# One level of Strassen's algorithm for gate and up of a SwiGLU in 17 of 22 blocks, with down blocks between a group's runs

## The chip, the cores and the metric

The kernel runs on one core of a Trainium2 chip. The metric is the device time of one execution in microseconds (us). Short names: PE is TensorE (matmuls), PEld its weight loads, DVE is VectorE, ACT is ScalarE, POOL is GpSimd, SP is the engine that issues the DMAs. PSUM is the memory that matmuls write to; one bank holds 128 x 512 float32.

## The reference, cut to what matters

One residual block over 512 tokens of width 1024 in float32. The change concerns the last two lines, the SwiGLU with its hidden width of 2816 and the final norm:

```python
def _rms(t, w):
    y = t * lax.rsqrt(jnp.mean(t * t, axis=-1, keepdims=True) + EPS)
    return y * w

def _swiglu(h, w_gate, w_up, w_down):
    return (jax.nn.silu(h @ w_gate) * (h @ w_up)) @ w_down

x = x + _mixer_block(_rms(x, norm_mix_w), ...)          # attention, gated linear attention
x = x + _memory_xattn(_rms(x, norm_mem_q_w), _rms(mem, norm_mem_kv_w), ...)
x = x + _swiglu(_rms(x, norm_ffn_w), w_ffn_gate, w_ffn_up, w_ffn_down)
return _rms(x, norm_final_w)
```

## The kernel before

**Layout.** All activations are transposed: features on the 128 partitions, the 512 tokens along the free axis. The residual stream is eight tiles `res[0]` to `res[7]` of 128 x 512 (named `x` in the profile). The hidden width is 22 blocks of 128 features.

**Two parts for each number.** Every float32 operand is split (`split`, lines 93 to 104) into a high part, a cast on ACT to the format that matmuls read, and a low part, the rest, a subtraction on DVE. `prod3` makes three matmuls of a product: high by high, high by low, low by high. A unit (`unit`) is a weight tile of 128 x 1024: a DMA brings it into `R`, ACT casts it to `H`, DVE leaves the rest in `L`. There are three buffers for each of the three, so the cast of a unit waits for the run that last read its buffer, and the DMA of a unit for the low part of the one three before.

**The FFN, lines 1008 to 1060.** For each hidden block j, `block` makes a run of 24 matmuls of 512 columns (8 blocks of the width by 3) for gate into the bank `pg`, and another run for up into `pu`. `ps_mm` has four banks, so a run can start when the bank of four runs ago has been read. The 1/rms of each token isn't in the operands `zh`, `zl`; it is multiplied in behind the matmuls by `n2.b`, a 128 x 512 tile with the same row in each partition (`rb` in the profile). So each block has on DVE L1022 (gate by 1/rms, out of PSUM), on ACT the Silu, on DVE L1024 (by up, out of PSUM) and L1025 (by 1/rms), and a split. The norm `n2` runs beside the first blocks: squares on ACT, their sums on DVE (L205), a matmul with ones (`t`), a chain of small operations on DVE for the inverse root (L216, L166 to L178; its end is `rt`), a matmul that spreads it over the partitions, and a copy on ACT into `rb`.

Behind the 22 blocks come the eight blocks of the down product, one for each `res[j]`: 66 matmuls of 512 columns each (22 by 3), an addition to `res[j]` (L1040), the squares for the final norm `n3`, and a product with the final gain. The last one is made in two halves of 256 tokens, each with its own `n3.finish` and its eight products into `fin` (L1052 to L1058; six on DVE, two on POOL), which go out by DMA. `finish` and its spread share a single PSUM bank (`ps_t`), and L1052 and L1058 read the spread from it.

**Order.** Each engine executes its own instructions in the order in which the program issues them; across engines they wait for each other through semaphores. The compiler's scheduler chose the order on each engine here.

Of the kernel before, what the change touches and what calls it, by code (L numbers as in the profile page):

```python
# [11 lines left out]
F32 = mybir.dt.float32  # L12
# [17 lines left out]
NEG = -1.0e30  # L30
TGW = 328
DENSE = (10, 5, 11, 3, 1)


def build(tc, a, out):
# [11 lines left out]
    cp = ctx.enter_context(pool("cp"))  # L47


    edge = ctx.enter_context(pool("ep", side="right")).tile([P, 24], F32, name="edge")  # L50
# [30 lines left out]
    def f(ap):  # L81
        return ap.bitcast(F32)
# [97 lines left out]
    class Norm:  # L180
# [23 lines left out]
            else:  # L204
                nc.vector.tensor_tensor(out=acc, in0=acc, in1=sq, op=ALU.add)  # L205

        def finish(self, spread=True, cols=None):
# [7 lines left out]
            v = cp.tile([P, nt], F32, name=uniq(f"v_{self.name}"))  # L215
            nc.vector.tensor_scalar(  # L216
                out=v, in0=ps[:, 0 : 2 * nt].rearrange("p (t c) -> p t c", c=2)[:, :, 0],
                scalar1=1.0 / D, scalar2=EPS, op0=ALU.mult, op1=ALU.add,
            )
# [785 lines left out]
    mep_ctx.__exit__(None, None, None)  # L1005


    fp_ctx = pool("fp")
    fp = fp_ctx.__enter__()
    ah = [fp.tile([P, S], F32R, name=f"ah{j}") for j in range(NF)]  # L1010
    al_ = [fp.tile([P, S], F32R, name=f"al{j}") for j in range(NF)]
    for j in range(NF):
        pg = ps_mm()
        block(pg, [(unit(a["w_fg"][j]), KC)], zh, zl)
        pu = ps_mm()
        block(pu, [(unit(a["w_fu"][j]), KC)], zh, zl)
        if j == 0:
            for i in range(KC):
                n2.add(res[i])
            n2.finish()  # L1020
# [5 lines left out]
        split(ah[j], al_[j], t)  # L1026

    n3 = Norm("n3", S)
    for j in range(KC):
        units = []  # L1030
        for k0 in range(0, NF, KC):
            nk_ = min(KC, NF - k0)
            units.append((unit(a["w_fd"][j][:, k0 * P : (k0 + nk_) * P]), nk_))
# [100 lines left out]
```

## Time and profile before

| | |
|---|---|
| time, median of 3 runs | 918.81 us (918.31 to 920.23) |
| the profiled execution's own time | 919.91 us |
| its span, first to last instruction | 918.1 us |
| mean granted TensorE clock | 0.995 |
| PE busy | 901.2 us, 98% of the span |
| DVE busy | 557.4 us, 61% |
| ACT busy | 426.5 us, 46% |
| first FFN matmul, end of the last gate or up run, start of the second half of the last block | 541.7, 783.2, 896.4 us |

The profile is of one execution; its times below are on its own clock, which starts with the first instruction. Busy times overlap between engines. A row of a timeline gives the start, the duration, the line, the operation and, in brackets, the idle time before it on its engine with what ended it. A duration of one instruction is longer than the distance to the next where instructions overlap; the distance between starts is called the pace here.

### The profile page before, as it was taken

The numbers are of one execution on the slowest core, as the hardware profiler recorded it, in microseconds if no ns is written. First come the engines' busy times: TensorE is split into PE (matmuls) and PEld (weight loads), VectorE is DVE, ScalarE is ACT, GpSimd is POOL, SyncE is SP. The second block draws the span as 40 slices with busy tenths as digits, with TensorE's granted clock in tenths as the row PEclk, the third lists the DMA queues.
The fourth block names the chain that finished last, engine by engine and source line by source line (L and its number), as shares of the span: only waits on it lengthen the run. The fifth ranks groups of instructions, "written<-read, shape, count | busy, mean of one in ns | idle before, by whom it ended". The sixth has DMA issues, their size and how long they took to land.

```text
span 918.1 us, 11424 instructions
## 1 busy us (share of the span) xinstructions
PE 901.2 (98%) x4318; PEld 746.7 (81%) x4318; DVE 557.4 (61%) x1104; ACT 426.5 (46%) x760; POOL 7.0 (1%) x30
## 2 busy tenths in 40 slices
PE   8999999999999999999999999999999999999995
PEld 6898888887888787778888778888888888888885
DVE  6777888777343959966766996444444444323323
ACT  7576574556333838463445864223332233222220
POOL 1000000000000000000000000000000000000001
PEclk9999999999999999999999999999999999999998
DMA  7232221222232031425432222232222322323212
GB/s 249 92 115 70 69 70 69 70 69 69 92 96 89 23 115 48 143 86 161 114 115 92 70 89 95 94 107 99 92 92 92 106 100 86 104 86 103 87 41 92
DMA packets 29415, 86.11 MB, mean 94 GB/s; under 512 B 4048, under 2 KB 7760, under 8 KB 29360
## 3 DMA queue, kind: packets, MB, share of 16 engines
q1 hardware_dynamic: 29216, 85.37, 28.9%
q8 instruction: 34, 0.56, 0.2%
q14 instruction: 21, 0.17, 0.1%
q10 hardware_dynamic: 144, 0.00, 0.0%
HBM read 83.27 MB, written 2.10 MB: 93 GB/s over the span
## 4 chain that ended last, share of the span: by engine, by line
PE 89%; DVE 6%; ACT 3%; DMA 1%; issue 1%; SPq 0%; DVEq 0%; ACTq 0%
PE mm L79 80%; PE s L79 3%; PE o L79 3%; PE t L79 1%; DVE L L98 1%; PE t L545 1%; ACT pm L93 1%; DMA R<-in_w_tg 1%; PE mm L545 1%; ACT H L97 1%; DVE sl L98 1%; DVE on L747 1%; DMA x<-in_xT 0%; PE t L758 0%; DVE st L706 0%
## 5 line engine op out<-in xcount | busy, mean ns | idle before, releaser
L97 ACT CAST H<-R 128x1024 fp32r<-128x1024 f32 (+2 forms) x155 | 156.8, 1013 | 326.1 <-PE mm L79 247.0
L98 DVE TENSOR_TENSOR L<-R,H 128x1024 fp32r<-128x1024 f32 (+2 forms) x155 | 181.8, 1174 | 93.9 <-ACT H L97 93.5
L79 PE MATMUL mm<-xl,H 128*128 128x512 f32 x592 | 232.3, 392 | 0.0
L79 PE MATMUL mm<-xh,L 128*128 128x512 f32 x592 | 232.1, 392 | 0.0
L79 PE MATMUL mm<-xh,H 128*128 128x512 f32 x592 | 230.6, 390 | 0.0
L79 PEld LDWEIGHTS mm<-xh,H 128*128 128x128 f32 x592 | 111.2, 188 | 22.5
L79 PEld LDWEIGHTS mm<-xl,H 128*128 128x128 f32 x592 | 111.2, 188 | 22.1
L79 PEld LDWEIGHTS mm<-xh,L 128*128 128x128 f32 x592 | 111.3, 188 | 21.7
L79 PE MATMUL mm<-ah,H 128*128 128x512 f32 (+1 forms) x198 | 72.5, 366 | 0.0
L79 PE MATMUL mm<-ah,L 128*128 128x512 f32 (+1 forms) x198 | 72.4, 366 | 0.0
L79 PE MATMUL mm<-al,H 128*128 128x512 f32 (+1 forms) x198 | 72.4, 365 | 0.0
L79 PE MATMUL mm<-H,xh 128*128 128x512 f32 (+1 forms) x192 | 70.3, 367 | 0.0
L79 PE MATMUL mm<-L,xh 128*128 128x512 f32 (+1 forms) x192 | 70.3, 366 | 0.0
L79 PE MATMUL mm<-H,xl 128*128 128x512 f32 (+1 forms) x192 | 70.1, 365 | 0.0
L1024 DVE TENSOR_TENSOR t2k<-t2k,mm 128x512 f32<-128x512 f32 x22 | 15.0, 687 | 68.3 <-PE mm L79 67.7
L93 ACT ACTIVATE p<-sm,nm,sc 128x256 f32<-128x256 f32 (+1 forms) x64 | 36.3, 569 | 25.4 <-DVE es L519 20.3
L1022 DVE TENSOR_TENSOR t2k<-mm,rb_n 128x512 f32<-128x512 f32 x22 | 15.1, 691 | 44.9 <-PE mm L79 43.0
L79 PEld LDWEIGHTS mm<-al,H 128*128 128x128 f32 x198 | 37.3, 189 | 6.1
L79 PEld LDWEIGHTS mm<-ah,H 128*128 128x128 f32 x198 | 37.3, 189 | 6.0
L79 PEld LDWEIGHTS mm<-ah,L 128*128 128x128 f32 x198 | 37.3, 189 | 6.0
L79 PEld LDWEIGHTS mm<-L,xh 128*128 128x128 f32 x192 | 36.1, 188 | 5.5 <-DVE L L98 0.6
L79 PEld LDWEIGHTS mm<-H,xh 128*128 128x128 f32 x192 | 36.3, 189 | 5.1 <-issue 0.2
(300 smaller groups left out, 1365.7 us busy)
## 6 DMA issues: line engine op xcount, KB each, us to landing
R<-in_w_fg SPq DMA_DIRECT2D x22, 512.0 KB, 3.2
R<-in_w_fu SPq DMA_DIRECT2D x22, 512.0 KB, 3.3
R<-in_w_gate SPq DMA_DIRECT2D x16, 512.0 KB, 3.3
R<-in_w_fd SPq DMA_DIRECT2D x16, 512.0 KB, 3.5
x<-in_xT SPq DMA_DIRECT2D x16, 256.0 KB, 3.5
R<-in_w_q SPq DMA_DIRECT2D x8, 512.0 KB, 3.5
R<-in_w_attn_o SPq DMA_DIRECT2D x8, 512.0 KB, 3.3
R<-in_w_vg SPq DMA_DIRECT2D x8, 512.0 KB, 3.3
```

Of the source, the lines that this page charges most:

```text
L79: nc.tensor.matmul(o, lhsT=lhsT, rhs=rhs, start=start, stop=stop)
L93: last_table[0] = nc.scalar.activation(*args, **kw)
L97: nc.scalar.copy(out=hi, in_=src)
L98: nc.vector.tensor_tensor(out=lo, in0=src, in1=f(hi), op=ALU.subtract)
L545: nc.tensor.transpose(out=pt[:, i * P : (i + 1) * P], in_=prs[i // 2][:, i % 2, b * P : (b + 1) * P], identity=ident)
L747: nc.vector.scalar_tensor_tensor(out=on[t][:, vs], in0=on[t][:, vs], scalar=r[:, h : h + 1], in1=glaw, op0=ALU.mult, op1=ALU.mult)
L1022: nc.vector.tensor_tensor(out=t, in0=pg, in1=n2.b, op=ALU.mult)
L1024: nc.vector.tensor_tensor(out=t, in0=t, in1=pu, op=ALU.mult)
```

## The change

The gate and up products of blocks 5 to 21 are made as 17 groups. In a group, gate and up together are a 2 x 2 product of blocks: the width in two halves of 512 features (by rows of the weights), gate and up (by columns of the weights), and the tokens in two halves of 256. Strassen's algorithm (in Winograd's form) makes it from 7 products of blocks in place of 8: `r11`, `r21`, `t2`, `t1`, `t3`, `r22`, `t4`, each 12 matmuls of 256 columns (4 by 3). Four of the products need sums of the weights, which `weight_side` forms on DVE for each group and splits (`SH`, `SL`, `DH`, `DL`), and four need sums of the tokens, which `sums` forms once and `splits` splits (`zt`). The results are put together on DVE, with three copies out of PSUM on ACT (`group`).

The first five blocks stay as they were, ten runs of 24 matmuls (runs 0 to 9). Beside them a table, `beside`, says in which order DVE and ACT do the other work; the order of these two is written by hand there, and that of PE in the groups. The down product is made in five parts, `PARTS`: between the products of the groups of one part stand the down blocks of the part before, with 15 or 12 matmuls of 512 columns, and the eight of the last part stand at the end, with 15 each, the last one in halves of 15 of 256 columns. All these are added to `res`.

The tokens lose 1/rms: `scale_stream` multiplies `res` by rms (the reciprocal of `n2.b`), the final norm's EPS is scaled to go with it, and the last product with `n2.b` of each block is gone.

```diff
+NPLAIN = 5
+PARTS = ((0, 5), (5, 9), (9, 13), (13, 17), (17, 22))
...
-    for j in range(NF):
-        pg = ps_mm()
-        block(pg, [(unit(a["w_fg"][j]), KC)], zh, zl)
-        pu = ps_mm()
-        block(pu, [(unit(a["w_fu"][j]), KC)], zh, zl)
...
-        nc.vector.tensor_tensor(out=t, in0=t, in1=n2.b, op=ALU.mult)
...
+    def sums(i):
+        tiles = [act_tile("zx") for _ in range(3)]
...
+            nc.vector.tensor_scalar_mul(x12[:, e], res[k][:, t1], wa)
+            stt(x1, res[k][:, t0], wa, x12, ALU.subtract)
+            stt(x2, res[q][:, t1], wb, x1, ALU.add)
+            stt(x3, res[q][:, t1], wb, x12, ALU.subtract)
+            stt(x4, res[q][:, t0], wb, x2, ALU.subtract)
...
+    def splits(i):
+        x1, x2, x3, x4 = token_sums[i]
+        for o, x, sign in (("t2", x2, -1.0), ("t1", x1, -1.0), ("t3", x3, None), ("t4", x4, -1.0)):
+            split(zt[o][:, 2 * i : 2 * i + 2, 0], zt[o][:, 2 * i : 2 * i + 2, 1], x, sign)
...
+    def scale_stream(js):
+        if js[0] == 0:
+            nc.vector.reciprocal(rms, n2.b)
+        for i in js:
+            nc.vector.tensor_tensor(out=res[i], in0=res[i], in1=rms, op=ALU.mult)
...
+        h = fw.tile([P, 1024], F32R, tag="SH", bufs=3, name=uniq("SH"))
+        lo = fw.tile([P, 1024], F32R, tag="SL", bufs=3, name=uniq("SL"))
+        split(h, lo, src)
...
+    def weight_side(j):
...
+        h0, l0 = pair_of(r0)
+        nc.vector.tensor_tensor(out=sa[:, 0], in0=r0[:, q1], in1=r1[:, q1], op=ALU.add)
+        nc.vector.tensor_tensor(out=sa[:, 1], in0=r1[:, q0], in1=r1[:, q1], op=ALU.add)
+        nc.vector.tensor_tensor(out=sb[:, 0], in0=sa[:, 1], in1=r0[:, q1], op=ALU.add)
+        nc.vector.scalar_tensor_tensor(
+            out=sb[:, 1], in0=sb[:, 0], scalar=-1.0, in1=r0[:, q0], op0=ALU.mult, op1=ALU.subtract
+        )
+        hb, lb = pair_of(sb.rearrange("p e c -> p (e c)"))
+        ha, la = pair_of(sa.rearrange("p e c -> p (e c)"))
+        hd, ld = (fw.tile([P, 512], F32R, tag=n, bufs=1, name=uniq(n)) for n in ("DH", "DL"))
+        split(hd, ld, r1[:, q0])
...
+    def group(j):
...
+        w = first_weights.pop() if first_weights else weight_side(j)
+        pa, pb = ps_mm()[:, :HS], ps_mm()[:, :HS]
+        g = t2k()
+        product(pa, w, "r11", True)
+        nc.scalar.copy(out=g[:, t0], in_=pa)
+        product(pb, w, "r21", True)
+        nc.vector.tensor_tensor(out=g[:, t0], in0=pb, in1=g[:, t0], op=ALU.add)
+        yield
+        pc = ps_s()[:, :HS]
...
+        product(pa, w, "t2", False)
+        nc.scalar.copy(out=g[:, t1], in_=pa)
+        product(pc, w, "t1", True)
+        product(pa, w, "t3", False)
+        nc.scalar.copy(out=s3, in_=pa)
+        nc.vector.tensor_tensor(out=s3, in0=pc, in1=s3, op=ALU.subtract)
+        yield
+        product(pc, w, "r22", False)
+        nc.vector.tensor_tensor(out=g[:, t1], in0=g[:, t1], in1=pc, op=ALU.subtract)
+        activation(g, j)
+        product(pa, w, "t4", False)
+        nc.vector.scalar_tensor_tensor(out=g[:, t0], in0=pa, scalar=-1.0, in1=g[:, t0], op0=ALU.mult, op1=ALU.mult)
+        nc.vector.tensor_tensor(out=g[:, t1], in0=s3, in1=g[:, t1], op=ALU.mult)
+        hidden(j, g)
...
+    def plain_act(j):
         t = t2k()
-        nc.vector.tensor_tensor(out=t, in0=pg, in1=n2.b, op=ALU.mult)
+        nc.vector.tensor_tensor(out=t, in0=outs[2 * j], in1=n2.b, op=ALU.mult)
         table_act(t, t, AF.Silu)
-        nc.vector.tensor_tensor(out=t, in0=t, in1=pu, op=ALU.mult)
...
+    beside = {
+        0: [lambda: squares(range(4))],
+        1: [lambda: squares(range(4, 8)), norm_2],
+        2: [lambda: sums(0), lambda: plain_act(0)],
+        3: [lambda: splits(0)],
+        4: [lambda: plain_act(1), lambda: sums(1)],
+        5: [lambda: splits(1)],
+        6: [lambda: plain_act(2), lambda: scale_stream(range(2))],
+        7: [lambda: scale_stream(range(2, KC))],
+        8: [lambda: plain_act(3), lambda: first_weights.append(weight_side(NPLAIN))],
+        9: [],
+    }
...
+        for i in range(2 * NPLAIN):
+            if i + 2 < 2 * NPLAIN:
+                us.append(unit(plain[i + 2]))
+            outs.append(ps_mm())
+            block(outs[i], [(us[i], KC)], zh, zl)
+            for do in beside[i]:
+                do()
...
+                g = group(j)
+                next(g)
+                if two == 2 and not late:
+                    down(p - 1, next(at))
+                next(g)
+                down(p - 1, next(at))
+                next(g)
+                if two == 2 and late:
+                    down(p - 1, next(at))
```

What moves on the engines is seen at three places. The first is on DVE, where the norm's chain ends (`rt`). Before, the next rows are the activations of the first two blocks, `mm_5457` and `mm_5573` being their gate banks:

```order
L178 SCALAR_TENSOR_TENSOR rt_n_1051_5548<-nwt_5550,nwy_5549 128x4
L1022 TENSOR_TENSOR t2k_5566<-mm_5457,rb_n_1055_5564 128x512
L1022 TENSOR_TENSOR t2k_5635<-mm_5573,rb_n_1055_5564 128x512
L1024 TENSOR_TENSOR t2k_5566<-t2k_5566,mm_5488 128x512
L1024 TENSOR_TENSOR t2k_5635<-t2k_5635,mm_5604 128x512
L1025 TENSOR_TENSOR t2k_5566<-t2k_5566,rb_n_1055_5564 128x512
L1025 TENSOR_TENSOR t2k_5635<-t2k_5635,rb_n_1055_5564 128x512
L98 TENSOR_TENSOR L_5714<-R_5712,H_5713 128x1024
L98 TENSOR_TENSOR al_5435<-t2k_5566,ah_5413 128x512
```

After, the low part of run 4's weights (`L_5553`) and the ten operations of `sums(0)` (`zx`) stand between the chain and the first activation, which reads the gate bank of block 0, `mm_5447`:

```order
L181 SCALAR_TENSOR_TENSOR rt_n_1057_5532<-nwt_5534,nwy_5533 128x4
L1189 TENSOR_SCALAR alr<-v_n_1056_5530 128x4
L101 TENSOR_TENSOR L_5553<-R_5551,H_5552 128x1024
L1057 TENSOR_SCALAR zx_5582<-x_0_4470,wf_w 128x256
L1055 SCALAR_TENSOR_TENSOR zx_5582<-x_0_4470,wf_w,zx_5582 128x256
L1055 SCALAR_TENSOR_TENSOR zx_5583<-x_4_4632,wf_w,zx_5582 128x256 x2
L1055 SCALAR_TENSOR_TENSOR zx_5584<-x_4_4632,wf_w,zx_5583 128x256
L1057 TENSOR_SCALAR zx_5582<-x_1_4509,wf_w 128x256
L1055 SCALAR_TENSOR_TENSOR zx_5582<-x_1_4509,wf_w,zx_5582 128x256
L1055 SCALAR_TENSOR_TENSOR zx_5583<-x_5_4673,wf_w,zx_5582 128x256 x2
L1055 SCALAR_TENSOR_TENSOR zx_5584<-x_5_4673,wf_w,zx_5583 128x256
L1178 TENSOR_TENSOR t2k_5595<-mm_5447,rb_n_1061_5548 128x512
```

The reading of the bank that run 4 needs has moved behind twelve instructions; before, it followed the chain at once.

The second is on DVE of the change, from the activation of block 2 (`mm_5647` is its gate bank) to the low part `L_5774` of run 9's weights, the last run ahead of the groups:

```order
L1178 TENSOR_TENSOR t2k_5762<-mm_5647,rb_n_1061_5548 128x512
L1180 TENSOR_TENSOR t2k_5762<-t2k_5762,mm_5698 128x512
L101 TENSOR_TENSOR a_5766<-t2k_5762,a_5766 128x512
L1073 RECIPROCAL rms<-rb_n_1061_5548 128x512
L1075 TENSOR_TENSOR x_0_4470<-x_0_4470,rms 128x512
L1075 TENSOR_TENSOR x_1_4509<-x_1_4509,rms 128x512
L101 TENSOR_TENSOR L_5774<-R_5772,H_5773 128x1024
L1075 TENSOR_TENSOR x_2_4550<-x_2_4550,rms 128x512
L1075 TENSOR_TENSOR x_3_4591<-x_3_4591,rms 128x512
```

A reciprocal of 128 x 512 and two of the eight products of `scale_stream` have come ahead of that low part; before, nothing but activations and low parts stood there.

The third is on ACT of the change, in the first group, j = 5. `SH_5847`, `SH_5855`, `SH_5859` and `DH_5863` are its own weights, `SH_6056` is the first cast of the next group's, `H_6028` and `H_6106` are down units; the two copies of `mm_5902` are those of `r11` and of `t2`:

```order
L100 CAST SH_5847<-R_5841 128x1024
L100 CAST H_6028<-R_6027 128x640
L100 CAST SH_5855<-SB_5844 128x1024
L100 CAST SH_5859<-SA_5843 128x1024
L100 CAST DH_5863<-R_5842 128x512
L100 CAST SH_6056<-R_6050 128x1024
L1140 COPY t2k_5904<-mm_5902 128x256
L96 ACTIVATE t2k_5892<-t2k_5892 128x512
L100 CAST H_6106<-R_6105 128x640
L100 CAST a_5896<-t2k_5892 128x512
L1147 COPY t2k_5904<-mm_5902 128x256
```

The copy of `r11`, for which the product `t2` waits (it goes on in the same bank), stands behind the next group's cast, and the copy of `t2`, for which `t3` waits, behind the cast of a down unit, a Silu and a cast. Before, there were no such copies.

## Rows read from the trace of the kernel before

**Rows 1.** The page of the profile: engines' busy time; the chain that ended last, by engine.
```profile
PE 901.2 (98%) x4318; PEld 746.7 (81%) x4318; DVE 557.4 (61%) x1104; ACT 426.5 (46%) x760; POOL 7.0 (1%) x30
...
PE 89%; DVE 6%; ACT 3%; DMA 1%; issue 1%; SPq 0%; DVEq 0%; ACTq 0%
```

**Rows 2.** Windows: start and end, length, busy time (instructions) by engine, clock, DMA share, GB/s.
```profile
541.70:564.00 22.30, 22.00 (x104) 17.95 (x103) 15.71 (x28) 10.08 (x14) 0.00 (x0) 1.00 0.34 115
564.00:783.20 219.20, 219.20 (x968) 181.53 (x968) 103.66 (x125) 68.34 (x85) 0.00 (x0) 1.00 0.29 96
...
896.40:918.10 21.70, 11.76 (x92) 11.14 (x90) 8.03 (x32) 1.58 (x4) 2.85 (x4) 0.80 0.29 97
```

**Rows 3.** Timeline of PE: start, duration, instruction; 156 and 41 in a row.
```profile
589.70 0.39 PE L79 MATMUL mm<-xh,L 128*128 128x512 f32 x1
...
624.83 0.39 PE L79 MATMUL mm<-xl,H 128*128 128x512 f32 x1
...
901.07 0.28 PE L79 MATMUL mm<-al,H 128*128 128x256 f32 x1
...
905.87 0.28 PE L79 MATMUL mm<-ah,L 128*128 128x256 f32 x1
```

**Rows 4.** Timeline of DVE around the first FFN blocks.
```profile
545.40 0.75 DVE L101 SCALAR_TENSOR_TENSOR xl<-x,wf_w,xh 128x512 fp32r<-128x512 f32 x1
546.06 0.69 DVE L205 TENSOR_TENSOR acc_n<-acc_n,sq 128x512 f32<-128x512 f32 x1
546.67 0.75 DVE L101 SCALAR_TENSOR_TENSOR xl<-x,wf_w,xh 128x512 fp32r<-128x512 f32 x1
547.33 1.22 DVE L98 TENSOR_TENSOR L<-R,H 128x1024 fp32r<-128x1024 f32 x1
548.46 0.69 DVE L205 TENSOR_TENSOR acc_n<-acc_n,sq 128x512 f32<-128x512 f32 x1
...
557.58 0.69 DVE L205 TENSOR_TENSOR acc_n<-acc_n,sq 128x512 f32<-128x512 f32 x1 [0.70 <-ACT sq L199]
```

**Rows 5.** Timeline of ACT, the same stretch.
```profile
556.92 0.63 ACT L199 ACTIVATE sq<-x 128x512 f32<-128x512 f32 x1 [0.76 <-DVE acc_n L205]
558.01 1.04 ACT L97 CAST H<-R 128x1024 fp32r<-128x1024 f32 x1 [0.47 <-PE mm L79]
563.56 0.59 ACT L228 COPY rb_n<-t 128x512 f32<-128x512 f32 x1 [4.50 <-PE t L79]
```

**Rows 6.** Chain of waits, 540 to 572 us: start, duration, what.
```profile
562.39 1.13 PE t L79 x8
```

**Rows 7.** Groups of DVE by line and form.
```profile
L539 DVE TENSOR_SCALAR p<-p,dn 128x256 f32<-128x256 f32 x48 | 13.7, 350 | 0.4
...
L706 DVE SCALAR_TENSOR_TENSOR st<-st,aend,s 128x256 f32<-128x256 f32 x28 | 12.9, 477 | 0.4
...
L536 DVE RECIPROCAL dn<-dn 128x4 f32<-128x4 f32 x16 | 2.9, 178 | 0.5
...
L898 DVE RECIPROCAL dn<-dn 128x2 f32<-128x2 f32 x8 | 1.3, 163 | 0.4 <-ACT pm L93 0.3
```

**Rows 8.** Timeline of DVE and PE at the end.
```profile
901.84 1.74 DVE L1058 TENSOR_TENSOR fin<-x,t 128x256 f32<-128x256 f32 x5
906.19 0.42 DVE L1040 TENSOR_TENSOR x<-x,mm 128x256 f32<-128x256 f32 x1 [2.61 <-PE mm L79]
...
907.17 0.38 PE L79 MATMUL t<-ones,sq 128*128 128x2 f32 x2 [0.90 <-ACT sq L199]
...
911.95 1.74 DVE L1058 TENSOR_TENSOR fin<-x,t 128x256 f32<-128x256 f32 x5
```

**Rows 9.** DMA issues: KB each, us from issue to landing.
```profile
R<-in_w_fd SPq DMA_DIRECT2D x8, 384.0 KB, 3.1
```

**Rows 10.** Timeline of PE at the start; windows near the end.
```profile
1.23 3.59 PE L79 MATMUL s<-t2k 128*128 128x512 bf16 x8 [1.23 <-DVE t2k L145]
...
909.90:911.20 1.30, 1.19 (x4) 0.91 (x4) 0.00 (x0) 0.05 (x1) 0.00 (x0) 0.50 0.00 0
```

More of the change, by code (lines that the diff above doesn't have):

```diff
@@ L47, in build @@
     cp = ctx.enter_context(pool("cp"))
-    edge = ctx.enter_context(pool("ep", side="right")).tile([P, 24], F32, name="edge")
+    ep_ctx = pool("ep", side="right")
+    edge = ep_ctx.__enter__().tile([P, 24], F32, name="edge")
     wp = ctx.enter_context(pool("wp"))
@@ L205, in add, with finish @@
                 nc.vector.tensor_tensor(out=acc, in0=acc, in1=sq, op=ALU.add)
-        def finish(self, spread=True, cols=None):
+        def finish(self, spread=True, cols=None, eps=None):
             cs = cols or self.all
@@ L214, in finish @@
                 terms(ps[:, 2 * t : 2 * t + 2], [(x[:, t * P : (t + 1) * P], ones[:, 0:2]) for x in parts])
[L215 to L219, printed above, removed]
+            v = self.v = cp.tile([P, nt], F32, name=uniq(f"v_{self.name}"))
+            sums = ps[:, 0 : 2 * nt].rearrange("p (t c) -> p t c", c=2)[:, :, 0]
+            if eps is None:
+                nc.vector.tensor_scalar(out=v, in0=sums, scalar1=1.0 / D, scalar2=EPS, op0=ALU.mult, op1=ALU.add)
+            else:
+                nc.vector.scalar_tensor_tensor(
+                    out=v, in0=sums, scalar=1.0 / D, in1=eps[:, cs.start // P : cs.stop // P], op0=ALU.mult, op1=ALU.add
+                )
             self.tok = cp.tile([P, nt], F32, name=uniq(f"rt_{self.name}"))
@@ L1005, in build @@
     mep_ctx.__exit__(None, None, None)
+    ep_ctx.__exit__(None, None, None)
+    HS = S // 2
+    t0, t1 = slice(0, HS), slice(HS, S)
     fp_ctx = pool("fp")
     fp = fp_ctx.__enter__()
-    ah = [fp.tile([P, S], F32R, name=f"ah{j}") for j in range(NF)]
-    al_ = [fp.tile([P, S], F32R, name=f"al{j}") for j in range(NF)]
-    for j in range(NF):
-        pg = ps_mm()
-        block(pg, [(unit(a["w_fg"][j]), KC)], zh, zl)
-        pu = ps_mm()
-        block(pu, [(unit(a["w_fu"][j]), KC)], zh, zl)
[L1017 to L1020, printed above, removed]
+    fe_ctx = pool("fe", side="right")
@@ new lines, in build, with act_tile, hidden, stt @@
+    fedge = fe_ctx.__enter__().tile([P, 8], F32, name="fedge")
+    nc.gpsimd.memset(fedge, 0.0)
+    fw_ctx = pool("fw", side="right")
+    fw = fw_ctx.__enter__()
+    act = {}
+    def act_tile(n):
+        return fp.tile([P, 2, S], F32R, tag="a", bufs=9, name=uniq(n))
+    def hidden(j, t):
+        act[j] = act_tile("a")
+        split(act[j][:, 0], act[j][:, 1], t)
+    zt = {o: fp.tile([P, 4, 2, HS], F32R, name=f"z_{o}") for o in ("t1", "t2", "t3", "t4")}
+    token_sums = {}
+    def sums(i):
+        tiles = [act_tile("zx") for _ in range(3)]
+        x12, x1, x2, x3, x4 = [f(x)[:, e].rearrange("p (k c) -> p k c", k=2) for x in tiles for e in range(2)][:5]
+        for e in range(2):
+            k, q = 2 * i + e, 4 + 2 * i + e
+            wa, wb = wf_w[:, k : k + 1], wf_w[:, q : q + 1]
+            def stt(o, x, w, y, op):
+                nc.vector.scalar_tensor_tensor(out=o[:, e], in0=x, scalar=w, in1=y[:, e], op0=ALU.mult, op1=op)
+            nc.vector.tensor_scalar_mul(x12[:, e], res[k][:, t1], wa)
[3 more added lines that the diff above has]
+            stt(x4, res[q][:, t0], wb, x2, ALU.subtract)
+        token_sums[i] = x1, x2, x3, x4
@@ new lines, in product, with activation @@
+    def product(o, w, op, first):
+        h, lo = w[op]
+        for k in range(4):
+            ks = slice(k * P, (k + 1) * P)
+            for i, (l_, r_) in enumerate(prod3(h[:, ks], lo[:, ks], *token_parts(op, k))):
+                nc.tensor.matmul(
+                    o, lhsT=l_, rhs=r_, start=first and k == 0 and i == 0, stop=k == 3 and i == 2,
+                    skip_group_check=not first,
+                )
+    def activation(g, j):
+        nc.vector.tensor_tensor(out=g, in0=g, in1=n2.b, op=ALU.mult)
+        table_act(g, g, AF.Silu)
@@ new lines, in group @@
+    def group(j):
[8 more added lines that the diff above has]
+        pc = ps_s()[:, :HS]
+        s3 = tp.tile([P, S], F32, tag="sq", bufs=1, name=uniq("s3"))[:, t0]
+        product(pa, w, "t2", False)
[12 more added lines that the diff above has]
+        hidden(j, g)
+        yield
@@ new lines, in down_units, with down_block, down @@
+    def down_units(p, i):
+        lo, hi = PARTS[p]
+        return [(unit(a["w_fd"][i][:, lo * P : hi * P]), hi - lo)]
+    def down_block(o, p, units, cs):
+        ks = range(*PARTS[p])
+        block(o, units, [act[k][:, 0, cs] for k in ks], [act[k][:, 1, cs] for k in ks])
+    def down(p, i):
+        units = down_units(p, i)
+        pd = ps_mm()
+        down_block(pd, p, units, slice(0, S))
+        nc.vector.tensor_tensor(out=res[i], in0=res[i], in1=pd, op=ALU.add)
+    def plain_act(j):
@@ L1021, in build, with squares @@
         t = t2k()
-        nc.vector.tensor_tensor(out=t, in0=pg, in1=n2.b, op=ALU.mult)
+        nc.vector.tensor_tensor(out=t, in0=outs[2 * j], in1=n2.b, op=ALU.mult)
         table_act(t, t, AF.Silu)
-        nc.vector.tensor_tensor(out=t, in0=t, in1=pu, op=ALU.mult)
-        nc.vector.tensor_tensor(out=t, in0=t, in1=n2.b, op=ALU.mult)
-        split(ah[j], al_[j], t)
+        nc.vector.tensor_tensor(out=t, in0=t, in1=outs[2 * j + 1], op=ALU.mult)
+        hidden(j, t)
+    def squares(js):
+        for i in js:
+            n2.add(res[i])
@@ new lines, in norm_2 @@
+    def norm_2():
+        n2.finish()
+        nc.vector.tensor_scalar_mul(eps, n2.v, EPS)
+    eps = alr[:, 0, 0:NT]
+    first_weights = []
+    beside = {
[9 more added lines that the diff above has]
+        9: [],
+    }
@@ new lines, in build @@
+    plain = [a[n][j] for j in range(NPLAIN) for n in ("w_fg", "w_fu")]
+    us = [unit(x) for x in plain[:2]]
+    outs = []
+    with tc.manual_schedule(engines={mybir.EngineType.DVE, mybir.EngineType.Activation}):
+        for i in range(2 * NPLAIN):
[5 more added lines that the diff above has]
+                do()
+        plain_act(NPLAIN - 1)
@@ new lines, in build @@
+    with tc.manual_schedule(engines={mybir.EngineType.PE}):
+        for p in range(1, len(PARTS)):
+            js = list(range(*PARTS[p]))
+            n = [KC // len(js)] * len(js)
+            for i in (-1, 0, 1, 2, 3)[: KC - sum(n)]:
+                n[i] += 1
+            at = iter(range(KC))
+            for j, two in zip(js, n):
+                late = j in (js[0], NF - 1)
+                g = group(j)
[7 more added lines that the diff above has]
+                    down(p - 1, next(at))
@@ L1028, in build @@
     n3 = Norm("n3", S)
     for j in range(KC):
[L1030 to L1033, printed above, removed]
+        units = down_units(len(PARTS) - 1, j)
         W = S if j < KC - 1 else S // 2
@@ L1038, in build @@
             pb = ps_mm()
-            block(pb[:, :W], units, [x[:, cs] for x in ah], [x[:, cs] for x in al_])
+            down_block(pb[:, :W], len(PARTS) - 1, units, cs)
             nc.vector.tensor_tensor(out=res[j][:, cs], in0=res[j][:, cs], in1=pb[:, :W], op=ALU.add)
@@ L1044, in build @@
                 continue
-            n3.finish(cols=cs)
+            n3.finish(cols=cs, eps=eps)
             for i in (7, 6, 0, 1, 2, 3, 4, 5):
@@ L1060, in build @@
                     nc.sync.dma_start(out[i // 2][:, :, cs], f3)
+    fw_ctx.__exit__(None, None, None)
+    fe_ctx.__exit__(None, None, None)
     fp_ctx.__exit__(None, None, None)
@@ L1121 @@
     }
+    w_fg, w_fu = arrays["w_fg"], arrays["w_fu"]
+    arrays["w_fgu"] = np.concatenate(
+        [w[NPLAIN:, :, c] for w in (w_fg, w_fu) for c in (slice(512, 1024), slice(0, 512))], 2
+    )
+    arrays["w_fg"], arrays["w_fu"] = w_fg[:NPLAIN], w_fu[:NPLAIN]
     nc = bacc.Bacc("TRN2", target_bir_lowering=False, num_devices=1)
```

21 lines of the change are left out of this document (added).

## The prediction, made before the change was run

> **What bounds the kernel now.** I read the page first: PE is busy for 98% of the span and the chain that ended last is 89% PE [rows 1]. Then the windows by stage: from 541.7 us, where the FFN starts, to 564.0 PE is busy for 22.00 of 22.30 us while the second norm is made beside it, and from there through the blocks for all of 219.20 us, with DVE busy for 103.66 [rows 2]. Only the tail, 896.4 to 918.1, has PE at 11.76 of 21.70. So a matmul less is worth its pace as long as PE stays fed, and everything that DVE and ACT do is free until PE waits for it. The timeline of PE gives the pace [rows 3]: 155 steps of 512 columns take 35.13 us, 0.2267 each; 40 steps of 256 columns take 4.80, 0.120 each, a little over half.
>
> **What the change removes.** A block has 48 matmuls of 512 columns, 48 x 0.2267 = 10.88 us; a group has 84 of 256, 10.08. 17 x 0.80 = 13.6 us. The down product keeps its matmuls, except that the halved block has 15 instead of 66 pairs of 256 columns: 51 x (2 x 0.120 - 0.2267) = 0.7. PE loses 14.3 us.
>
> **The tail gives some back.** The last half's matmuls were cover for the first half's norm and output. From the end of the first half's matmuls, 896.4, to the end take 21.7 us [rows 2]. In that time the first half's products end at 901.84 + 1.74 = 903.58, 7.2 later, and the second half's addition (0.42) now falls among them: 7.6. The second half's sum needs the bank that those products read, so it starts there, and from its start, 907.17, to the end take 10.9 [rows 8]. 7.6 + 10.9 = 18.6 with rounding. The halved block's matmuls shrink by 51 x 0.120 = 6.1, the tail by 3.1 only: +3.0. Net so far -11.3.
>
> **Where PE now waits: the passage from the runs to the groups.** The table puts the token sums, their splits, the scaling of `res` and the first weight side on DVE and ACT in about 70 us. I followed DVE's and ACT's new order from 547.9 us by the paces before. On DVE, from the distances of starts: a product of 512 columns 0.61, one with a scalar 0.66, a low part of 1024 1.13; an operation that needs the other engine's answer in order idles 0.70 [rows 4]. On ACT a 512-wide cast or square takes 0.63, a 1024-wide cast 1.04 [rows 5]. A 256-wide scalar operation takes 0.35 or 0.48 (0.27 and 0.40 as paces, 0.08 less as in rows 4) [rows 7]: the ten of `sums` come to 4.2 with 0.12 more for each that reads the one before it. An activation with its split is three products and two waits, 3.4; four low parts of `splits` 2.6.
>
> - *Run 4.* PE gets there at 565.9 (a wait of 0.3 for `rt` behind it). It needs the bank of run 0, which waits for: `rt` at 560.9; its spread, 1.13 [rows 6], and the copy, 0.59, to 562.9; the cast of run 4's weights, which stands behind that copy on ACT, to 563.8; the low part to 565.0; the ten sums to 569.2; the first product to 569.9. **4.0 us.** Before, that product followed the copy, which ended at 564.15 [rows 5].
> - *Run 9.* From 569.2: first activation and unit 4.9, four low parts and unit 3.7, second activation 3.4, sums 4.2, unit, low parts, unit 4.9, third activation 3.4: 593.7. Then the reciprocal, two products 1.2 and the low part 1.2. PE needs that part after two matmuls, at 597.6. The trace has no reciprocal of 512 columns. With 4 columns it takes 178 ns and with 2 163 ns [rows 7]: 7.5 ns a column, 4.0 us for 512; the other bound is the 0.69 of a tensor operation of this width. I take the slope, since it is the same operation. The low part ends at 600.2: **2.6 us**; at 0.69 no wait.
> - *Start of the first group.* Six more products 3.6 to 603.7, the fourth activation 2.65 to its cast, then the cast of the group's first weights to 607.4, while PE would start at 605.2: 2.25. Two matmuls later it needs the low part: 1.0 more. **3.3 us.**
> - *`t2` of the first group.* The four weight sums end at 612.0, ACT's casts of them at 614.5, the next group's cast at 615.4 and only then the copy of `r11`, 615.8, where PE is due at 611.4: **4.5 us.**
> - *`t3`.* Its copy stands behind the cast of a down unit. That unit's DMA needs the buffer freed at 616.1 on DVE and lands 3.1 us later [rows 9]; cast, Silu's split and copy end at 620.8 for 618.7: **2.1 us.**
>
> Together 16.8 (13.5 with a cheap reciprocal: the first group then waits 2.6 in place of 3.3). For this DVE has 50.0 us of work up to `t2`'s low part and PE 53.2 before `t2`: it is not that DVE is too slow, it is in the wrong order, and idles 16 us waiting for ACT and the chain.
>
> The reciprocal has a rule too. By the Trainium skill ("VectorE: DVE Perf Modes", "First, the fixed hardware budget") Reciprocal is an iterative divide with a repeat count of 8. An estimate from it, eight times the slope of a low part, (1.13 - 0.61)/512 us a column, gives 4.2 us in place of 4.0 and so 2.8 for run 9; no row here shows a wide one.
>
> **Where PE may wait in each group.** By the paces above DVE has in a group four low parts (4.0), four weight sums (2.5), seven operations that put the results together (2.9) and 0.3 between those that read each other, with 1.3 for each down block: 11.0 us with one and 12.3 with two, where PE has 10.08 + 2.7 = 12.8 and 15.5 (16.9 with blocks of 15). It keeps up on average. One place is tight: after `t3` ends, ACT casts part of the next group's weights into the buffer that `t3` has freed, DVE takes its low part, and only then subtracts what `r22` needs: 0.2 + 1.04 + 1.13 + 0.42 + 0.1 = 2.9. The down block between is 12 x 0.2267 = 2.7: 0.2 in each of the 12 groups with a part of four, **2.0 us** (0 to 4).
>
> **The clock.** PE's start, after no work, shows 3.59 us for 8 matmuls of 512 columns, 0.45 each or half the rate [rows 10, 3]; near the end, where it waits for the second half's norm, the granted clock is 0.50, the lower level, 1.2 GHz [rows 10]. The waits of 4.0 and 4.5 us may bring that too. A stretch like the first costs 1.8. What it costs behind run 4 is taken out of run 9's wait. I put **1.8** in for the first group (0 to 3.6).
>
> **Sum.** -14.3 + 3.0 + 16.8 + 2.0 + 1.8 = +9.3, against the profiled execution's 919.91 (span 918.1, and 1.8 around it) 929.2; against the median, 1.1 below it, 918.8 + 9.3 = **928.1**. Its own bounds: reciprocal -3.3, groups and clock -3.8 or +3.8: 921 to 932. A measurement here can tell some 0.2%, 1.8 us, from no change.
>
> **The rivals.**
> - *PE is fed throughout.* Then only the matmuls and the tail count: -11.3, **907.5**. For it: DVE's 50.0 of 53.2 us. Against: the order, fixed by hand, with 0.70 idle at each answer from ACT [rows 4]. It ends below the time before where all waits stay under 11.3 us, half of mine. 0.13.
> - *Cheap reciprocal, no wait in the groups, no fall of the clock.* -11.3 + 13.5 = +2.2, **921.0**; half of its spread lies within 0.2%. For it: no row shows a wide reciprocal or a group. 0.12.
> - *The clock falls at each long wait and nothing absorbs it.* The gaps at run 4, the group's start, `t2`, each 1.8, or 5.4 for 1.8: +12.9, **931.7**. For it: half rate at the start and 0.50 at the end [rows 10]; against: the start's wait had no work before it at all. 0.15. The Trainium skill says the same ("TensorE: Matmul & The Clock Gate", "HAM oscillation — how this bites in real kernels"): idle gaps between runs of matmuls put the array back to its lower clock, so short runs lose more than the gap. The 0.50 after the tail's gap agrees.
> - *DVE becomes the bound in the groups.* With 12.3 of work and six or seven answers from ACT at 0.70 it would have 17 in place of 15.5 to 16.9, 1 us a group: 928.1 + 15, **943**. Against: in an order by hand other work stands between question and answer. 0.05.
> - My own sum: 0.55.
>
> **Numbers.** 928.1. The range runs from 918 (most of the cheap case) to 934 (clock case and the upper bounds); left out are the fed case, the DVE case and a few edges, 0.2. Faster by over 0.2% 0.13; within 0.08 (half of the cheap case and the edge of the others); slower 0.79.
>
> **What would show it.** Right: PE's timeline has gaps of 4.0 ahead of run 4, 2.6 in run 9, 3 at the first group's start, 4.5 ahead of its `t2`, 2 ahead of `t3`, some 16 us in all between 560 and 622, each ended by the instruction named; the reciprocal takes 4 us; from then on the groups lie at 10.1 us plus their down blocks with gaps of tenths; the tail from the first half's last matmul takes 18.6. Wrong: PE without gaps there (first rival), or gaps in every group (last), or 256-column matmuls at more than 0.120, 0.001 of which costs 1.4 us.

## The result: 0.85% slower, and where the time lies

The changed kernel takes 927.16 us (median of 4 runs, 926.06 to 927.82) against 919.29 us (918.31 to 920.23) of the kernel before, run beside it: a ratio of 1.0085, 95% interval 1.0067 to 1.0102. The profiled execution took 926.71 us, 6.8 more than that of before. The page of the profile after has these lines in the place of [rows 1]:

```profile
PE 892.9 (97%) x4879; PEld 761.5 (82%) x4879; DVE 674.4 (73%) x1338; ACT 476.6 (52%) x869; POOL 7.1 (1%) x31
...
PE 70%; DVE 15%; DMA 7%; ACT 5%; issue 2%; SPq 0%; DVEq 0%; ACTq 0%
```

PE is busy for 8.3 us less and the span is 6.8 longer: its work shrank and its waits grew by more. DVE's share of the chain that ended last went from 6 to 15%. The list of what PE waited for from the FFN on (in all, times, longest) names the places:

```profile
PE mm L82 <- DVE t2k L1178: 3.9, 1, 3.9
PE t L82 <- DVE rt_n L181: 3.4, 2, 1.9
PE t L82 <- DVE fin L1267: 2.7, 1, 2.7
PE mm L1125 <- ACT t2k L1140: 2.7, 1, 2.7
PE s L1125 <- DVE s L1151: 2.2, 3, 1.1
PE mm L1125 <- ACT SH L100: 1.9, 1, 1.9
PE mm L1125 <- DVE SL L101: 0.8, 1, 0.8
PE mm L1125 <- ACT t2k L1147: 0.2, 1, 0.2
```

The first is run 4 waiting for run 0's bank, the second the tail's two spreads (before, only the second of them waited), the third the tail's second sum, the fourth `t2` for the copy of `r11`, the fifth `r22` in the later groups, the sixth and seventh the first group's start, the last `t3` in a later group (769.1). The timeline of DVE shows what stands ahead of the first: the low part of run 4's weights, which waited for ACT, the ten sums, and then the product that frees the bank, as forecast for 569.2:

```profile
563.71 1.23 DVE L101 TENSOR_TENSOR L<-R,H 128x1024 fp32r<-128x1024 f32 x1 [2.80 <-ACT H L100]
564.85 0.35 DVE L1057 TENSOR_SCALAR zx<-x,wf_w 128x256 f32<-128x256 f32 x1
565.24 1.80 DVE L1055 SCALAR_TENSOR_TENSOR zx<-x,wf_w,zx 128x256 f32<-128x256 f32 x4
566.95 0.35 DVE L1057 TENSOR_SCALAR zx<-x,wf_w 128x256 f32<-128x256 f32 x1
567.33 1.80 DVE L1055 SCALAR_TENSOR_TENSOR zx<-x,wf_w,zx 128x256 f32<-128x256 f32 x4
569.05 0.68 DVE L1178 TENSOR_TENSOR t2k<-mm,rb_n 128x512 f32<-128x512 f32 x1
...
593.02 3.35 DVE L1073 RECIPROCAL rms<-rb_n 128x512 f32<-128x512 f32 x1
...
597.62 1.22 DVE L101 TENSOR_TENSOR L<-R,H 128x1024 fp32r<-128x1024 f32 x1
```

What the forecast had only as a separate term is the clock. PE's timeline behind run 4's wait and where run 9 first reads its low part, and windows of the same stretch and of the first group (columns as in [rows 2]):

```profile
569.88 0.77 PE L82 MATMUL mm<-xh,H 128*128 128x512 f32 x1 [3.87 <-DVE t2k L1178]
570.44 0.63 PE L82 MATMUL mm<-xl,H 128*128 128x512 f32 x1
...
575.13 0.40 PE L82 MATMUL mm<-xh,H 128*128 128x512 f32 x1
...
600.10 0.39 PE L82 MATMUL mm<-xh,L 128*128 128x512 f32 x1
```

```profile
569.90:575.60 5.70, 5.70 (x15) 4.46 (x15) 4.24 (x6) 4.95 (x8) 0.00 (x0) 0.54 0.12 24
575.60:605.00 29.40, 29.40 (x131) 24.22 (x129) 25.38 (x38) 8.96 (x14) 0.00 (x0) 1.00 0.25 79
605.00:615.50 10.50, 5.14 (x26) 4.41 (x24) 8.41 (x11) 6.06 (x8) 0.00 (x0) 0.84 0.40 130
615.50:620.30 4.80, 4.65 (x25) 4.45 (x25) 4.80 (x9) 2.15 (x4) 0.00 (x0) 0.64 0.25 71
```

From 569.88 to 575.13 twelve steps take 5.25 us where 2.72 were due: 2.5 us lost at the lower level. PE came that much later to run 9, and run 9 had no wait left: its low part was done at 598.84 and PE read it at 600.10, so that 1.2 of the 2.5 took the place of a wait there and the other 1.3 shortened the wait at the first group's start.

For all kernels of this study the FFN can be cut at three starts in the timelines: the first FFN matmul, the first matmul of the first group's `t3`, and the addition of the last block's first half (L1040 before, L1249 after; 896.56 before). The time from the first to the second is the passage, then the groups, then the tail up to the end of the span. Without any wait the passage is 240 x 0.2267 + 48 x 0.120 and 2.1 for the norm's own matmuls, 62.3 us.

| | passage | groups | tail | median | ratio to before |
|---|---|---|---|---|---|
| before | | | 21.5 | 919.29 | |
| the change | 78.3 | 284.9 | 19.7 | 927.16 | 1.0085 (1.0067 to 1.0102) |
| run 0's bank first | 77.3 | 287.6 | 19.5 | 926.54 | 1.0072 (1.0058 to 1.0085) |
| scaling late | 70.2 | 285.0 | 19.5 | 918.19 | 0.9989 (0.9981 to 0.9998) |
| group order | 76.7 | 285.6 | 19.5 | 925.55 | 1.0065 (1.0053 to 1.0078) |
| tail bank | 78.0 | 284.4 | 16.5 | 924.03 | 1.0046 (1.0034 to 1.0059) |
| 1/rms kept | 73.9 | 284.0 | 19.5 | 921.34 | 1.0026 (1.0013 to 1.0038) |
| refilled | 62.1 | 286.6 | 16.5 | 908.45 | 0.9884 (0.9868 to 0.9900) |
| refilled, group order | 62.2 | 286.4 | 16.5 | 907.81 | 0.9874 (0.9859 to 0.9889) |

### The profile page after: what moved, and what is told of

The parts are those of the page before. It is cut to its first block, busy times and chain, and to the rows that moved or that the text cites. A ratio compares the mean times of both kernels' runs of the same rounds, so it can differ in the third digit from the quotient of the medians.

```text
span 924.9 us, 12952 instructions
## 1 busy us (share of the span) xinstructions
PE 892.9 (97%) x4879; PEld 761.5 (82%) x4879; DVE 674.4 (73%) x1338; ACT 476.6 (52%) x869; POOL 7.1 (1%) x31
## 4 chain that ended last, share of the span: by engine, by line
PE 70%; DVE 15%; DMA 7%; ACT 5%; issue 2%; SPq 0%; DVEq 0%; ACTq 0%
PE mm L82 52%; PE mm L1125 7%; DMA R<-in_w_fd 4%; PE s L1125 3%; PE s L82 3%; PE o L82 3%; DVE L L101 2%; DMA R<-in_w_fgu 2%; DVE SL L101 2%; ACT H L100 1%; PE t L82 1%; PE t L551 1%; DVE zx L1055 1%; DMA R<-in_w_tg 1%; ACT pm L96 1%
## 5 line engine op out<-in xcount | busy, mean ns | idle before, releaser
L100 ACT CAST H<-R 128x1024 fp32r<-128x1024 f32 (+4 forms) x137 | 123.8, 905 | 175.8 <-PE mm L82 120.4
L101 DVE TENSOR_TENSOR L<-R,H 128x1024 fp32r<-128x1024 f32 (+4 forms) x137 | 142.5, 1042 | 53.1 <-ACT H L100 52.5
L82 PE MATMUL mm<-xh,H 128*128 128x512 f32 x320 | 125.7, 394 | 3.9 <-DVE t2k L1178 3.9
L82 PE MATMUL mm<-xl,H 128*128 128x512 f32 x320 | 127.4, 398 | 0.0
L82 PE MATMUL mm<-xh,L 128*128 128x512 f32 x320 | 127.2, 398 | 0.0
L82 PE MATMUL mm<-a,H 128*128 128x512 f32 (+1 forms) x362 | 110.2, 386 | 0.0
L82 PEld LDWEIGHTS mm<-a,H 128*128 128x128 f32 x362 | 65.3, 188 | 11.4
L82 PEld LDWEIGHTS mm<-xl,H 128*128 128x128 f32 x320 | 60.8, 190 | 11.7
L82 PEld LDWEIGHTS mm<-xh,L 128*128 128x128 f32 x320 | 60.8, 190 | 11.1
L82 PE MATMUL mm<-a,L 128*128 128x512 f32 (+1 forms) x181 | 69.3, 383 | 0.0
```

The lines of the kernel that those rows point to most:

```text
L82: nc.tensor.matmul(o, lhsT=lhsT, rhs=rhs, start=start, stop=stop)
```

## Experiments

**Run 0's bank first.** Is each wait due to the instruction that ends it, or are they one chain?

```diff
-        2: [lambda: sums(0), lambda: plain_act(0)],
+        2: [lambda: plain_act(0), lambda: sums(0)],
```

> Only the first activation (the reading of run 0's bank) is put ahead of the ten token sums on DVE. Theory: the passage is one chain through DVE and ACT, and a wait taken away at one place comes back at the next. Run 4's wait of 4.0 us goes, but run 5, run 7 and run 9 then wait about 2 us each for their low parts, because the same work is ahead of them on DVE; the first group starts at nearly the same time. 0.4 us less than the changed kernel, some 926.8. Rival: each wait belongs to the instruction that ends it. Then the 4.0 us at run 4 and the 2.7 us that PE loses behind it at half rate are saved: 6.7 us less, some 920.5.

Measured: 926.54 us, 0.6 less than the change, which can't be told from no difference (the intervals of the two ratios overlap). The wait at run 4 is gone, and PE waits elsewhere. Two lines of what PE waited for in this kernel, and windows behind two of its new waits and in the first group:

```profile
PE mm L1125 <- ACT t2k L1140: 4.7, 2, 4.4
PE mm L82 <- DVE L L101: 4.3, 3, 1.8
```

```profile
572.60:585.00 12.40, 11.29 (x49) 9.05 (x50) 10.87 (x20) 5.49 (x9) 0.00 (x0) 1.00 0.28 85
585.00:597.50 12.50, 11.06 (x48) 8.82 (x48) 11.08 (x13) 3.27 (x5) 0.00 (x0) 1.00 0.27 84
...
613.00:618.00 5.00, 4.89 (x23) 4.89 (x24) 5.00 (x9) 2.20 (x5) 0.00 (x0) 0.50 0.27 69
```

Three waits for low parts came up, of which the longest is 1.8, and the passage is 1.0 shorter. The rival is out. (The groups, whose code is the same, took 2.7 longer in this execution; with the tail bank, also the same code there, they took 0.6 less. PE's waits in them are 4.5 us in all for 2.6, so 1.9 of the 2.7; why they differ wasn't settled. So a difference of under 3 us between the groups of two profiled executions tells nothing by itself.) The windows show the clock as well: behind waits of under 2 us it stays at 1.00, and behind the 4.4 at `t2` it is at 0.50; at the first group's start, with the same two waits as in the change (1.9 and 0.8), it is at 1.00 here (604.70 to 611.00). So the 2.5 us that the clock took behind run 4 were saved here, and PE only waited longer for the same chain.

**Scaling late.**

```diff
-        6: [lambda: plain_act(2), lambda: scale_stream(range(2))],
-        7: [lambda: scale_stream(range(2, KC))],
+        6: [lambda: plain_act(2)],
+        7: [],
...
         units = down_units(p, i)
+        if p == 0:
+            with tc.issue_after(prev["s3"].ins):
+                scale_stream([i])
         pd = ps_mm()
```

(`prev["s3"]` is the current group's subtraction for `r22`, L1151 in the change.)

> The reciprocal and the eight products that scale the residual stream leave the passage; each tile is scaled right ahead of its first down addition, behind the first group's subtraction for r22. Theory (one chain): DVE has 3.35 + 8 x 0.61 = 8.2 us less ahead of the first group, and 0.7 of an idle place is gained; run 4 still waits 4.0, run 9 and the group's start no longer, t2 at most 2.7 and t3 not: 9 us less than the changed kernel, some 918. The groups with the down blocks of the first part have the slack for it (12.3 of 16.9 us). Rival: in the trace of the changed kernel no wait is ended by the reciprocal or by a scaling, so they cost nothing: no difference, some 927.

Measured: 918.19 us, 9.0 less, as the chain said; of the waits forecast, run 4 has 3.9, `t2` 1.3, and run 9, the group's start and `t3` none. The passage is 8.1 shorter, although the change's trace has no wait that the reciprocal ends; the groups, which took the work over, are no longer. Work that no wait names can lie on the path, if it stands in order ahead of what a wait does name.

**Group order.** The next group's first cast goes behind the copy of `r11`, its second behind the copy of `t3`, the low part of that behind the subtraction for `r22`.

```diff
-        h0, l0 = pair_of(r0)
+        with behind("c11"):
+            h0, l0 = pair_of(r0)
...
-        hb, lb = pair_of(sb.rearrange("p e c -> p (e c)"))
+        with behind("c3"), behind("s3"):
+            hb, lb = pair_of(sb.rearrange("p e c -> p (e c)"))
```

(`behind(n)` queues what it encloses behind the previous group's instruction n on the same engine.)

> In the groups the next group's weights go behind what PE waits for: on ACT the first cast behind the copy of r11 and the second behind the copy of t3, on DVE its low part behind the subtraction that r22 needs. Theory: the waits at r22 (some 3.5 us over the groups, 1.1 and 0.9 the longest) come from that order and go; the first t2 waits 1 us less, of which t3 takes half back: 4 us less than the changed kernel, some 923. Rival: the long waits at r22 come from the DMA of a down unit, for which the cast ahead of it on ACT waits: then they stay, at t2 or in the next products, and 0.5 to 1 us is saved, some 926.3.

Measured: 925.55 us, 1.6 less, between the two; the intervals of the ratios overlap, so that the 1.6 is hardly clear of noise. The passage gained 1.6, the groups nothing that can be told. In the change's trace one of the long waits at `r22` reads so, on ACT and on DVE:

```profile
738.85 0.62 ACT L100 CAST H<-R 128x512 fp32r<-128x512 f32 x1 [2.33 <-DMA R<-in_w_fd]
739.38 1.04 ACT L100 CAST SH<-SB 128x1024 fp32r<-128x1024 f32 x1
```

```profile
739.50 0.69 DVE L101 TENSOR_TENSOR L<-R,H 128x512 fp32r<-128x512 f32 x1 [2.19 <-ACT H L100]
740.45 1.23 DVE L101 TENSOR_TENSOR SL<-SB,SH 128x1024 fp32r<-128x1024 f32 x1 [0.25 <-ACT SH L100]
741.59 0.41 DVE L1151 TENSOR_TENSOR s<-s,s 128x256 f32<-128x256 f32 x1
```

A down unit's DMA holds up ACT, ACT the next group's cast, and that the subtraction behind the low part. In the new order all three waits at `r22` are gone, and `t2` waits in later groups for the copy of `r11`: 1.2, 0.7 and 0.8 us at 744.9, 807.4 and 851.8. On DVE a weight sum of a later group starts late there, ahead of the activation, just behind the landing of its weights (the trace has the DMA issued at 737.46 and landed 4.0 us later):

```profile
741.57 0.69 DVE L1109 TENSOR_TENSOR SA<-R,R 128x512 f32<-128x512 f32 x1 [1.79 <-issue]
```

That the DMA is the root is argued from these rows; a kernel with more buffers for the weights was not tried.

**Tail bank.**

```diff
-            n3.finish(cols=cs, eps=eps)
+            n3.finish(cols=cs, eps=eps, bank=ps_s if c0 else None)
```

> The second half of the last block makes its sum and its spread in another PSUM bank, so that they needn't wait for the first half's products. Theory (the tail's give-back is the wait for that bank, 2.7 us on PE): the second half's sum starts 2.8 us earlier, but its chain then shares DVE with the first half's products, and 1.3 us are left, some 925.9. Rival: the order on DVE decides, the second chain stands behind the first half's products anyway: no difference, or slower by the small operations that now stand ahead of them.

Measured: 924.03 us, 3.1 less, and the tail is 3.2 shorter; 1.3 were expected. The timelines of PE, of the change and then of this kernel, show the rest:

```profile
912.93 0.56 PE L82 MATMUL t<-ones,acc_n 128*128 128x2 f32 x2 [2.72 <-DVE fin L1267]
913.35 0.57 PE L82 MATMUL t<-ones,sq 128*128 128x2 f32 x2
```

```profile
907.97 0.38 PE L82 MATMUL s<-ones,sq 128*128 128x2 f32 x2 [0.90 <-ACT sq L202]
908.22 0.36 PE L82 MATMUL s<-ones,acc_n 128*128 128x2 f32 x2
```

Counted from the first half's addition, DVE has the sum 5.1 us earlier (4.55 behind the addition, at 908.84, for 9.61, at 914.81), where the expectation had 2.8. Its matmuls have the step of the higher level, 0.25 us, in place of 0.43: in the change PE was at the lower level already when it came to the wait of 2.7, as two windows of the change show.

```profile
904.00:909.50 5.50, 4.04 (x32) 3.71 (x32) 2.75 (x12) 2.11 (x4) 0.00 (x0) 1.00 0.00 0
909.70:912.90 3.20, 0.51 (x3) 0.22 (x2) 2.13 (x6) 0.37 (x1) 1.41 (x2) 0.50 0.03 11
```

The second chain does share DVE with the first half's products, as expected: they stand in its middle, from 909.90 to 912.03, and 1.9 of the 5.1 are lost.

**1/rms kept.** Of the change, the part that takes 1/rms out of the tokens is undone.

```diff
+        nc.vector.tensor_tensor(out=g, in0=g, in1=n2.b, op=ALU.mult)
...
+        nc.vector.tensor_tensor(out=t, in0=t, in1=n2.b, op=ALU.mult)
...
-        nc.vector.tensor_scalar_mul(eps, n2.v, EPS)
...
-            n3.finish(cols=cs, eps=eps)
+            n3.finish(cols=cs)
```

(the first in `group`, the second in `plain_act`; `scale_stream` is not called)

> The tokens keep 1/rms, as before the change: no reciprocal, no scaling of the residual stream, the plain EPS, and one more product of 512 columns with n2.b in each block; the Strassen groups stay. Theory (one chain in the passage, DVE with slack in the groups): 8.2 us leave the chain and four such products, 2.4, come into it, so that some 5 us of the passage are saved; the 17 products more in the groups are 0.6 of 12.8 to 16.9 us each and lengthen only the places that are already tight, some 2 us. 3 us less than the changed kernel, some 924. Rival: DVE is close to its bound in the groups, so each product more costs its 0.6 us: 5 less and 10 more, some 932.

Measured: 921.34 us, 5.8 less than the change. The passage is 4.3 shorter, near the 5 expected, and the groups, with 17 products more, are no longer (284.0 for 284.9). The rival's 10 us there did not come, and PE waits in them for 1.2 us in place of 2.6; the 2 us of the expectation are too few to be told from one execution, but the median, 5.8 less where 3 were expected, leaves no room for them. DVE is not near its bound there.

**Refilled.** The late scaling, the tail bank, and the table in a new order.

```diff
...
+        1: [lambda: squares(range(4, 8)), norm_2, lambda: sums(0, (0,)), lambda: gate(0)],
+        2: [lambda: silu(0), lambda: sums(0, (1,)), lambda: high(0, "t2", "t1"), lambda: up(0), lambda: low(0, "t2", "t1"), lambda: rest(0)],
+        3: [lambda: high(0, "t3", "t4"), lambda: low(0, "t3", "t4")],
+        4: [lambda: gate(1), lambda: silu(1), lambda: sums(1, (0,)), lambda: up(1), lambda: sums(1, (1,)), lambda: rest(1)],
+        5: [lambda: high(1, "t2", "t1", "t3", "t4"), lambda: low(1, "t2", "t1")],
+        6: [lambda: gate(2), lambda: silu(2), lambda: low(1, "t3"), lambda: up(2), lambda: low(1, "t4"), lambda: rest(2)],
+        7: [],
...
```

(`gate`, `silu`, `up` and `rest` are the steps of `plain_act`, `high` and `low` those of `splits` on ACT and on DVE; `sums(i, (e,))` makes one half of the sums.)

> The late scaling and the second bank in the tail together, and the passage in a new order: half of the first token sums go into DVE's idle time behind the norm's chain, the first activation's reading of the bank right behind them, and the other sums and low parts between the steps of an activation, where DVE waited 0.7 us for ACT. Nothing is added or left out. Theory: the chain loses the 9.0 and 3.1 us that the two parts gave alone, and the 4.0 at run 4 and most of the 1.3 at t2 too, with the clock's loss behind run 4 (2.7, until now hidden in later waits): some 4.5 to 6 us more. 910.5, below the kernel before. Rival: what is filled in delays the steps themselves (the Silu's answer is used later), and waits of 1 to 2 us come up at runs 5, 7 and 9 as when the bank was read first: then only the two parts add up, some 915.

Measured: 908.45 us, 18.7 less than the change and 1.16% less than before (interval 1.00 to 1.32%). The passage takes 62.1 us, what the matmuls alone need. The new order was not run without the other two parts; what it gave, 18.7 - 9.0 - 3.1 = 6.6, is a difference. All that PE still waits for from the FFN on:

```profile
PE s L82 <- DVE rt_n L181: 3.2, 1, 3.2
PE s L1136 <- DVE s L1162: 2.6, 5, 1.2
PE s L82 <- ACT sq L202: 0.9, 1, 0.9
PE mm L1136 <- ACT t2k L1151: 0.7, 2, 0.4
PE mm L1136 <- ACT t2k L1158: 0.4, 2, 0.2
```

**Refilled, group order.**

```diff
+        with behind(prev2, "ga"):
+            nc.vector.tensor_tensor(out=sa[:, 0], in0=r0[:, q1], in1=r1[:, q1], op=ALU.add)
```

(beside the edit of the third experiment; `prev2["ga"]` is the activation's product on DVE two groups earlier)

> As the one before, with the groups' order of the third experiment, and the weight sums of the group after next behind the activation of this one on DVE, since in the third experiment such a sum, waiting for its DMA, held up the activation and then the copy of r11. Theory: the waits in the groups, some 3 us, fall to 2 or less: 1 to 2 us less than the one before, some 909. Rival: the DMA of the weights comes late whatever the order (its buffers are freed late), and the wait only moves: the same as the one before.

Measured: 907.81 us, 0.6 less than the one before with overlapping intervals, so not told from it. The waits in the groups are 3.6 us in all where they were 3.7: `t2` and `t3` wait where `r22` did. The rival holds for what is left there.

## Why the prediction was right, step by step

**The matmuls saved.** Forecast 14.3 us from 0.120 a step of 256 columns. In the groups the step is 0.118 or 0.113 (below), so the products from the first `t3` to the last down blocks of the groups, 1380 matmuls, took 162.2 us with their small waits, not the 165.6 of the forecast: some 3 us more were saved.

**The passage.** Forecast 16.8 of waits and 1.8 of clock; measured 78.3 - 62.3 = 16.0. The waits stand where they were put: 4.0 at run 4 (3.9), 3.3 at the group's start (1.9 + 0.8), 4.5 at `t2` (2.7). Two are missing, 2.6 at run 9 and 2.1 at `t3` (0.1). At run 9 the low part was done 1.4 us ahead of the forecast, 0.65 of it by the cheaper reciprocal, so that about half of that wait was never due; the other half is time that PE had lost to the clock. `r11` and `r21`, and then `t2` and `t1`, ran for the most part at the lower clock too and lost some 1.5 us each time, most of what is missing at `t2` and at `t3`. The step that failed is the one that adds 1.8 for the clock in the first group: what PE loses ahead of a wait for the chain shortens that wait and costs nothing. The forecast had this for run 4 and not for the first group. The first experiment shows the same from the other side.

**The reciprocal.** Forecast 4.0 us from the slope of 2 and 4 columns, 7.5 ns a column; it takes 3.35, 6.5 ns. The estimate by the Trainium skill ("VectorE: DVE Perf Modes", "First, the fixed hardware budget"), 4.2, was high by more. The trace bears out that it is several times dearer than a tensor operation (0.69); how it is made the trace doesn't show.

**The groups.** Forecast 2.0 us of waits, one of 0.2 in each of 12 groups. By what the down block ahead of `r22` takes over its usual 2.75 they came to some 3.4, most of it in two of 1.3 and 1.1, by a cause that the forecast lacked, a down unit's DMA. The place was right, the size and its spread not. The down blocks' own pace, 2.75 for 12 in place of 2.72, adds 0.8 in all.

**The tail.** Forecast 3.0 given back; from the first half's addition to the end it was 21.5 and is 19.7, so of 6.1 us of matmuls 4.3 were given back. The mis-sized term is the second half's chain, taken as long as before (10.9) and measured as 12.0. The forecast counted it from 907.17 [rows 8], where the second of the sum's four rows of matmuls starts; the first had started at 905.99, ahead of the wait. In the change all four stand behind the wait for the bank, and at the lower clock: from the start so counted to DVE's first answer it takes 1.88 us, for 0.87 before.

**The sum.** -2.6 in the passage, -1.2 in the groups (258.9 us to the end of their last down block for 165.6 + 92.5 + 2.0), +1.3 in the tail, together 2.5 less than the forecast's +9.3; the profiles differ by 6.8, the medians by 7.9. Against the profile the sum is 2.5 off, and against the median, 928.1 for 927.16, only 0.9. That it came so near, with terms off by 1 to 3 us both ways (in the groups -3.4 for the matmuls, +1.4 for the waits and +0.8 for the down blocks), is partly luck.

**The rivals.** "PE is fed throughout" was 907.5; the refilled kernel, which feeds it in the passage, takes 908.45. But it has the second bank too, which gave 3.1 alone and isn't in that rival's price; without it some 911.6 would be left (an estimate from the two medians). So in the passage only the order stood between the change and that rival; in the groups PE still waits for 3.7 us, and the rival's whole price was not reached by order alone. "Cheap reciprocal" is refuted by the 3.35 us. "The clock falls at each long wait and nothing absorbs it" would have made the passage 16.8 + 5.4 longer than its matmuls; it is 16.0. The rule of the Trainium skill beside it ("TensorE: Matmul & The Clock Gate", "HAM oscillation — how this bites in real kernels") agrees with the windows as to the fall behind run 4 (0.54) and, in the first experiment, at `t2` (0.50). Behind the shorter waits of that experiment the clock stayed at 1.00, and what a fall costs in the end is decided by what PE waits for next. "DVE becomes the bound in the groups" is refuted by the kernel that keeps 1/rms: 17 products more on DVE, and no longer groups.

## What to carry to other kernels

Where an engine executes in order, follow its whole order from one wait of the bottleneck to the next, and count a chain once: taking one wait away moved it (0.6 us of 4.0 came off), taking work out of the chain that no wait named gave 9.0, and filling idle time inside the chain gave the rest. A saving in matmuls (here 1.2% of the time, net of the tail) shows only if the work that prepares it is spread so that the bottleneck never waits for it; and matmuls taken away at the end of a kernel are worth less than their time, if they covered a chain.

## What was not expected of the hardware

The same matmul of 256 columns has three paces at a granted clock of 1.00: 0.120 us in the tail before [rows 3], and in the change 2.83 us for 24 (0.118, from 697.16 to 699.99) or 2.72 (0.113, from 712.60 to 715.32). The quicker pace starts behind an `r22` whose own twelve matmuls took 1.47 to 1.49 us in place of 1.41, and lasts up to the next down block: from 837.50 to 845.66, for one, six products take 1.36 each. So it is in 11 of the 17 groups; in five `r22` took 1.41 and `t4` behind it kept 0.118, and in one it took 1.52 and `t4` kept 0.118 too. What sets the pace stays open.

And the clock: in the change it was at 0.50 before run 4's wait of 3.9 us was over, in the first group from 2 us behind its start on, and there once more behind `t2`'s wait of 2.7; in the tail it fell just behind a wait of 1.5 for the first half's norm, ahead of the wait of 2.7. In the first experiment it stayed at 1.00 behind three waits of 1.1 to 1.8 us with a run of 24 matmuls between them, and behind the same two waits at the group's start (1.9 and 0.8), and fell during `t2`'s 4.4. So the same waits brought a fall in one execution and none in another, and the length of a wait alone doesn't tell.
